# Three rounded passes for the scores and weighted sums of two layers, and norms shifted on ScalarE over whole tiles

## The chip, the cores and the metric

The kernel runs on one core of a Trainium2 chip. Its time is the device time of one launch in microseconds (us). TensorE (PE) multiplies matrices out of SBUF into the eight banks of PSUM. VectorE (DVE) and ScalarE (ACT) work elementwise on SBUF and PSUM, and both also empty the banks. SyncE (SP) issues the transfers from and to HBM. Every engine works through its own instructions in order, and semaphores tie the engines together.

## The reference

Four layers act on 256 latent tokens and 256 context tokens, 2048 wide: Fourier mixing, a bidirectional mLSTM with 8 heads, grouped-query attention with 16 heads on 4 key heads, and Fourier mixing again. Everything is in 32 bits. The parts that the change touches are, in short:

```
hx = rmsnorm(x, g) * (1 + scale) + shift        # before each layer, for both streams
# layer 1, mLSTM: per head (128 wide q, k; 256 wide v)
s   = (q @ k.T) * exp(decay - m)                # scores with decays
num = s @ v                                     # weighted sum of values
h   = num / max(|sum s|, exp(-m));  y = rmsnorm(sigmoid(o) * h) * silu(z)
# layer 2, attention: only the latent queries are needed
p   = softmax(q @ k.T / sqrt(128));  y = (p @ v) * silu(z)
```

## The kernel before, in words

**The large matmuls.** `gemm` multiplies the 16 blocks of 128 rows of the activations with a weight block of 512 columns. Each 32-bit number is split into a rounded part and the rest, both in the type fp32r (`h` and `l` for activations, `wh` and `wl` for weights). One product is then three passes: `h*wh`, `h*wl`, `l*wh` (line 308). For weights ScalarE makes the rounded part (L266) and VectorE the rest (L267). Work that is written as F32 on PE, without the split, is one matmul in the program and two instructions on the engine.

**Order of the work.** PE's order is the order of the program text. The other engines' order is set by a scheduler that looks at the program's dependences. `Weave` mixes small work into the large matmuls: `run(gemm(...), fr, br, ar)` gives `fr` steps of the generator queue `fill` and `br` steps of `bg` for each step of the gemm. A gemm's step is mostly the 6 passes of one of its blocks with two blocks of activations; a generator's step is its code up to the next `yield`. `fill.finish(key)` runs what is left at once. `bg` holds the products that make the layers' modulation vectors on VectorE (`ada_dve`, L227, 1024 columns each, about 1.2 us).

**Buffers.** The gemms use four PSUM banks (`acc`), one for each of their four blocks. A gemm's last step finishes its blocks one after the other, `done(b, ...)` empties bank `b`, and the next gemm needs bank `b` when it comes to its block `b`. The small work shares the other four banks (`xb`).

**Layer 1** works on four pairs of heads. Each pair has four gemms with the evictions `done_qk`, `done_v`, `done_o`, `done_z`. The first two are one ScalarE copy for a bank. `core` runs in the steps of the third and fourth gemm: for each of 8 tiles, `stage_a` computes the scores on PE (L846) and applies the decays on VectorE and ScalarE, `stage_b` turns the result on PE (L882) and copies it (`wt`), and `stage_c` multiplies it with the values (L891). `stage_a` runs one tile ahead. `finish` of a pair normalises, turns, and stores `zs` to HBM (L977) while the next pair's first gemm runs.

**Layer 2** has the gemms k, v, four q, four z. `qk_norm` normalises and rotates q or k and turns it (L1082) after four steps' wait. `attend` works on 8 tiles per key head: `stage_a` scores (L1097), a row maximum on VectorE (L1099), exponentials on ScalarE (L1103); `stage_b` turns (L1109) and `stage_c` multiplies with the values (L1118).

**Norms between layers.** `Norm.make` gives block `kt` of the next layer's input. `modulate` does it for one stream, 256 columns: VectorE scales (L405), ScalarE adds the shift and rounds (L406), VectorE makes the rest (L407). The first four blocks are made stream by stream, the other twelve for both.

Of the kernel before, what the change touches and what calls it, by code (L numbers as in the profile page):

```python
# [14 lines left out]
P = 128  # L15
# [9 lines left out]
NPE1, CORE1, ATT = 4, 0.4, 1.2  # L25
# [24 lines left out]
def _build(tc, nc, top, A, out):  # L50
# [360 lines left out]
    class Norm:  # L411
# [20 lines left out]
        def make(self, kt, s=None, have=None):  # L432
            for s in range(2) if s is None else (s,):
                have = modulate(self.l, kt, self.rn[kt // 4][:, kt % 4, 256 * s:256 * s + 256], self.rows[s],
                                self.pp, s, have)
            return have
# [304 lines left out]
    with ExitStack() as st:  # L741
        p1 = pool(st, "l1", reuse_waits="tile")

        def w2(name):
            return p1.tile([P, 512], F32, tag="w2", name=name, bufs=5)
# [6 lines left out]
        def gates():  # L752
# [21 lines left out]
            sb = pY.tile([P, 4, 512], F32, tag="zs", name="sb", bufs=1)  # L774
            ri, rl, rb, rM, z0 = sa[:, 0, :], sa[:, 1, :], sa[:, 2, :], sa[:, 3, :], sb[:, 0, :]
# [25 lines left out]
            for n, src in enumerate((ri, rM, rb)):  # L801
                r = sb[:, n + 1, :]
# [21 lines left out]
        def core(c):  # L824
# [16 lines left out]
            def stage_a(hh, i, ub, um):  # L841
# [4 lines left out]
                T.matmul(sp[:, :ns], c.qk[:, hh, dg], c.qk[:, 2 + hh, :ns], start=True, stop=True)  # L846
# [31 lines left out]
            def stage_b(hh, i, big):  # L878
                ns = 256 if i < 2 else 512
                pt = bank()  # L880
                for k in range(ns // 128):
                    T.transpose(pt[:, 128 * k:128 * k + 128], big[:, 128 * k:128 * k + 128], ident)  # L882
                wt = p1.tile([P, 512], F32, tag="wt", name="wt", bufs=2)
                S.copy(wt[:, :ns], pt[:, :ns])
                return wt

            def stage_c(hh, i, wt):
                nb = 2 if i < 2 else 4
                po = bank()
                for k in range(nb):  # L890
                    T.matmul(po[:, :256], wt[:, 128 * k:128 * k + 128], c.v[:, k, 256 * hh:256 * hh + 256],  # L891
                             start=k == 0, stop=k == nb - 1)
                ys = c.yp[:, i, 256 * hh:256 * hh + 256]
                if c.pend is not None:
                    S.copy(ys, po[:, :256])
                    c.pend.append((hh, i))
                else:
                    c.gate(hh, i, po[:, :256])
# [3 lines left out]
            w = {0: stage_a(0, 0, *u[0])}  # L902
            yield
            for n, (hh, i) in enumerate(tiles):
                if n == 2:
                    u[1] = load(1)
                if n + 1 < 8:
                    h2, i2 = tiles[n + 1]
                    w[n + 1] = stage_a(h2, i2, *u[h2])
                    yield  # L910
                if n:
                    stage_c(*tiles[n - 1], wt)
                    yield
# [24 lines left out]
        def make_pair(p):  # L938
            c = Pair()
            c.p = p  # L940
            c.qk = p1.tile([P, 4, 512], F32, tag="qk", name="qk", bufs=1)
            c.v = p1.tile([P, 4, 512], F32, tag="v", name="v", bufs=1)
            c.to = p1.tile([P, 4, 512], F32, tag="to", name="to", bufs=1)
            c.ssq = pY.tile([P, 8], F32, tag="ssq", name="ssq", bufs=2)
            c.pend = []

            def gate(hh, i, src):
                ys = c.yp[:, i, 256 * hh:256 * hh + 256]
                V.scalar_tensor_tensor(ys, c.to[:, i, 256 * hh:256 * hh + 256], 1.0, src, ALU.add, ALU.mult)  # L949
                jk = p1.tile([P, 256], F32, tag="jk", name="jk", bufs=1)  # L950
                S.activation(jk, ys, AF.Square, accum_out=c.ssq[:, 4 * hh + i:4 * hh + i + 1])  # L951

            c.gate = gate

            def done_qk(b, ps):
                S.activation(c.qk[:, b, :], ps, AF.Copy, scale=128 ** -0.5 if b < 2 else 1.0)

            def done_v(b, ps):
                S.copy(c.v[:, b, :], ps)

            def done_o(b, ps):
                S.activation(c.to[:, b, :], ps, AF.Tanh, scale=0.5)
                if b == 3:
                    pend, c.pend = c.pend, None
                    for hh, i in pend:
                        gate(hh, i, c.yp[:, i, 256 * hh:256 * hh + 256])
# [26 lines left out]
        for p in range(4):  # L993
# [9 lines left out]
            c.zs = pY.tile([P, 4, 512], F32, tag="zs", name="zs", bufs=1)  # L1003
# [38 lines left out]
    with ExitStack() as st:  # L1042
# [45 lines left out]
        def done_k(b, ps):  # L1088
            fill.add("kT", qk_norm(ps, 1, b - 2 if b >= 2 else None, kT[:, :, 128 * b:128 * b + 128]))
# [4 lines left out]
        def attend(g, qT, o):  # L1094
# [34 lines left out]
            yield  # L1129
# [31 lines left out]
        for g in range(4):  # L1161
            qT = p2.tile([P, 4, 256], F32, tag="qT", name="qT", bufs=2)
# [251 lines left out]
```

## Time and profile before

| | us |
|---|---|
| median of 3 runs | 2126.71 (2125.92 to 2127.11) |
| the profiled execution | 2128.92 |
| its span, first to last instruction | 2127.1 |
| PE busy in the span | 2083.3 |
| DVE, ACT busy | 1508.7, 817.8 |

A row with a window gives, for each engine, the busy time and in brackets the number of instructions. A row of the timeline gives the start and the duration in us, the engine, the line, and what is written and read. A matmul's duration reaches past the start of the next, because matmuls overlap in the array; what one costs is read from start to start. "x2" on a row of the timeline stands for two instructions in a row. A row of a group ends with the busy time of the group, the mean of one in ns, and the engine's idle time just before them with what ended it.

### The profile page before, as it was taken

To read this page: it belongs to the slowest core of one execution; us is meant where nothing else is said; L and a number is where in the kernel's file an instruction comes from. 1 tells how busy PE (TensorE), PEld (TensorE's weight loads), DVE (VectorE), ACT (ScalarE), POOL (GpSimd) and SP (SyncE) were. 2 spreads that over 40 slices of the span, in tenths; PEclk is the share of its full clock that TensorE was granted. 3 is DMA by queue.
4 is the path that set the end of the run, shared out by engine and by line. 5 is a ranking of instruction groups with operands and counts; after the bars stand their busy time and mean duration, and the time that the engine had idled before them with its cause. 6 is when DMAs were issued, how large, how long until landed. Compare 5 with 4: busy or idle time off the path is not lost. (4 is left out here: it accounts for less than half of the span.)

```text
span 2127.1 us, 29564 instructions
## 1 busy us (share of the span) xinstructions
PE 2083.3 (98%) x11292; PEld 1727.8 (81%) x11292; DVE 1508.7 (71%) x2761; ACT 817.8 (38%) x1342; POOL 20.4 (1%) x29
## 2 busy tenths in 40 slices
PE   7999999999999999999999999999999999999997
PEld 5678777797788888888888888888778777999986
DVE  6478888748787887798666768856545665657666
ACT  5442232224343324323332343223346554555443
POOL 0000000000000000000000000000000000000000
PEclk9999999999999999999999999999999999999999
DMA  9966878852554675477577778973243454564454
GB/s 395 333 242 210 293 256 302 323 191 96 179 188 163 221 244 169 162 272 248 186 240 262 236 239 299 334 288 107 89 148 111 151 176 131 184 194 136 150 198 148
DMA packets 127422, 451.51 MB, mean 212 GB/s; under 512 B 14368, under 2 KB 16928, under 8 KB 124592
## 3 DMA queue, kind: packets, MB, share of 16 engines
q1 hardware_dynamic: 126992, 448.71, 61.5%
q8 instruction: 88, 1.44, 0.3%
q10 hardware_dynamic: 288, 0.92, 0.1%
q14 instruction: 54, 0.44, 0.1%
HBM read 435.91 MB, written 13.66 MB: 211 GB/s over the span
## 5 line engine op out<-in xcount | busy, mean ns | idle before, releaser
L267 DVE TENSOR_TENSOR wl<-wraw,wh 128x1024 fp32r<-128x1024 f32 x400 | 489.1, 1224 | 405.5 <-ACT wh L266 398.2
L308 PE MATMUL acc<-h,wh 128*128 128x512 f32 (+1 forms) x1936 | 689.1, 356 | 6.6 <-ACT h L406 3.9
L266 ACT CAST wh<-wraw 128x1024 fp32r<-128x1024 f32 x400 | 419.3, 1049 | 701.2 <-PE acc L308 553.5
L308 PE MATMUL acc<-l,wh 128*128 128x512 f32 (+1 forms) x1936 | 671.4, 347 | 2.1 <-DVE l L407 1.8
L308 PE MATMUL acc<-h,wl 128*128 128x512 f32 (+1 forms) x1936 | 669.7, 346 | 0.1
L308 PE MATMUL acc<-wh,h 128*128 128x512 f32 x1024 | 426.8, 417 | 3.5 <-DVE xn L1062 2.2
L308 PEld LDWEIGHTS acc<-h,wh 128*128 128x128 f32 x1936 | 366.9, 190 | 66.3 <-issue 13.8
L308 PEld LDWEIGHTS acc<-l,wh 128*128 128x128 f32 x1936 | 366.7, 189 | 51.3 <-DVE l L407 3.5
L308 PEld LDWEIGHTS acc<-h,wl 128*128 128x128 f32 x1936 | 367.2, 190 | 44.0 <-issue 1.9
L308 PE MATMUL acc<-wh,l 128*128 128x512 f32 x1024 | 400.8, 391 | 0.5 <-DVE l L407 0.5
L308 PE MATMUL acc<-wl,h 128*128 128x512 f32 x1024 | 399.2, 390 | 0.0
L227 DVE SCALAR_TENSOR_TENSOR araw<-araw,cb 128x1024 f32<-128x1024 f32 x288 | 350.9, 1226 | 14.4 <-DMA araw<-in_ada_t_dram 12.1
L308 PEld LDWEIGHTS acc<-wh,h 128*128 128x128 f32 x1024 | 192.6, 188 | 51.8 <-issue 14.5
L308 PEld LDWEIGHTS acc<-wl,h 128*128 128x128 f32 x1024 | 192.8, 188 | 44.5 <-issue 8.4
L308 PEld LDWEIGHTS acc<-wh,l 128*128 128x128 f32 x1024 | 192.3, 188 | 42.7 <-DVE l L407 1.3
L227 DVE SCALAR_TENSOR_TENSOR ajunk<-araw,cb 128x1024 f32<-128x1024 f32 x160 | 195.6, 1223 | 0.0
L197 PE MATMUL xb<-araw,cpad 128*32 128x256 f32 x696 | 48.5, 396 | 4.4 <-ACT wh L266 2.6
L406 ACT ACTIVATE h<-mu,ada 128x256 fp32r<-128x256 f32 x80 | 36.9, 502 | 35.9 <-DVE mu L405 35.9
L891 PE MATMUL xb<-v,wt 128*128 128x256 f32 x192 | 46.8, 379 | 0.0
L464 ACT ACTIVATE sq<-rn 128x256 f32<-128x256 f32 (+1 forms) x48 | 24.7, 516 | 55.6 <-DVE rn L458 53.8
L951 ACT ACTIVATE jk<-yp 128x256 f32<-128x256 f32 x32 | 13.3, 416 | 79.8 <-DVE yp L949 79.8
L891 PEld LDWEIGHTS xb<-v,wt 128*128 128x128 f32 x192 | 36.4, 189 | 6.1
(231 smaller groups left out, 1480.3 us busy)
## 6 DMA issues: line engine op xcount, KB each, us to landing
araw<-in_ada_t_dram SPq DMA_DIRECT2D x288, 512.0 KB, 5.3
wraw<-in_w1in_dram SPq DMA_DIRECT2D x128, 512.0 KB, 4.3
araw<-in_ada_p_dram SPq DMA_DIRECT2D x87, 512.0 KB, 6.9
wraw<-in_w2in_dram SPq DMA_DIRECT2D x80, 512.0 KB, 3.5
wraw<-in_w0g_dram SPq DMA_DIRECT2D x32, 512.0 KB, 6.2
wraw<-in_w0o_dram SPq DMA_DIRECT2D x32, 512.0 KB, 6.1
wraw<-in_w1o_dram SPq DMA_DIRECT2D x32, 512.0 KB, 6.0
wraw<-in_w2o_dram SPq DMA_DIRECT2D x32, 512.0 KB, 4.1
```

The costliest lines, as they stand in the source:

```text
L197: T.matmul(ps[32 * q:32 * q + 32, :256], cpad[:, 4 * kq + q, :], rv[q // 2][:, 256 * (q % 2):256 * (q % 2) + 256], start=kq == 0, stop=kq ...
L227: V.scalar_tensor_tensor(o, rv, 1.0, cb[:, v + 2 - nv, part], ALU.mult, ALU.mult, accum_out=am[:, v, i, hf:hf + 1])
L266: S.copy(wh, raw)
L267: pace.append(V.tensor_tensor(wl, raw, wh.bitcast(F32), ALU.subtract).ins)
L308: T.matmul(o, lhsT, rhs, start=start, stop=stop)
L406: S.activation(h[:, c], u, AF.Identity, bias=ada[:, l, SH, s, kt:kt + 1])
L464: S.activation(sq[:, c], rn[:, b, c], AF.Square)
L891: T.matmul(po[:, :256], wt[:, 128 * k:128 * k + 128], c.v[:, k, 256 * hh:256 * hh + 256], start=k == 0, stop=k == nb - 1)
L951: S.activation(jk, ys, AF.Square, accum_out=c.ssq[:, 4 * hh + i:4 * hh + i + 1])
```

## The change

1. **Layer 1.** `done_qk` and `done_v` make, after ScalarE's copy, the rest on VectorE (`ql`, `vl`, 512 columns). Scores are three rounded passes in place of one F32 matmul, and so is each product of `stage_c`; `stage_b` therefore makes the rest `wtl` too. `stage_a` runs two tiles ahead, and `CORE1` is 0.56 steps instead of 0.4. `ql` shares its place with `zs`, so it waits for the store of the pair before, and `zs` for the end of this pair's `core`. The gate is written into `yp` itself.
2. **Layer 2.** `kT` and `qT` become rounded, their rests go to the context halves of input tiles in `hl` that are not read any more (`spare`), and a score is two passes of 512 columns and two of 256. Turning q waits six steps, a key head's second tile two steps more, and `ATT` is 1.35. The product with the values stays F32.
3. **Norms.** For the last twelve blocks VectorE multiplies by the row factor alone (256 columns), ScalarE applies scale and shift on the same place, then rounds 512 columns, and VectorE makes the rest of 512 columns.

```diff
-NPE1, CORE1, ATT = 4, 0.4, 1.2
+NPE1, CORE1, ATT = 4, 0.56, 1.35
...
         def make(self, kt, s=None, have=None):
...
+            u = self.pp.tile([P, 512], F32, tag="mu2", name="mu2", bufs=2)
+            for s in range(2):
+                c = slice(256 * s, 256 * s + 256)
+                V.tensor_tensor(u[:, c], self.rn[kt // 4][:, kt % 4, c], self.rows[s], ALU.mult)
+                S.activation(u[:, c], u[:, c], AF.Identity, scale=ada[:, self.l, SC, s, kt:kt + 1],
+                             bias=ada[:, self.l, SH, s, kt:kt + 1])
+            return split_into(kt, u)
...
-                T.matmul(sp[:, :ns], c.qk[:, hh, dg], c.qk[:, 2 + hh, :ns], start=True, stop=True)
+                for ip, (q, k) in enumerate(((c.qk, c.qk), (c.qk, c.ql), (c.ql, c.qk))):
+                    T.matmul(sp[:, :ns], q[:, hh, dg], k[:, 2 + hh, :ns], start=ip == 0, stop=ip == 2)
...
                 S.copy(wt[:, :ns], pt[:, :ns])
-                return wt
+                V.tensor_tensor(wtl[:, :ns], pt[:, :ns], wt[:, :ns].bitcast(F32), ALU.subtract)
+                return wt, wtl
...
-                    T.matmul(po[:, :256], wt[:, 128 * k:128 * k + 128], c.v[:, k, 256 * hh:256 * hh + 256],
-                             start=k == 0, stop=k == nb - 1)
+                    for ip, (w, v) in enumerate(((wt[0], c.v), (wt[0], c.vl), (wt[1], c.v))):
+                        T.matmul(po[:, :256], w[:, 128 * k:128 * k + 128], v[:, k, 256 * hh:256 * hh + 256],
+                                 start=k + ip == 0, stop=k == nb - 1 and ip == 2)
...
             def done_qk(b, ps):
-                S.activation(c.qk[:, b, :], ps, AF.Copy, scale=128 ** -0.5 if b < 2 else 1.0)
+                if b == 0:
+
+                    fill.finish(f"fin{p - 1}")
+                    c.ql = pY.tile([P, 4, 512], F32R, tag="zs", name="ql", bufs=1)
+                sc = 128 ** -0.5 if b < 2 else 1.0
+                S.activation(c.qk[:, b, :], ps, AF.Copy, scale=sc)
+                V.scalar_tensor_tensor(c.ql[:, b, :], ps, sc, c.qk[:, b, :].bitcast(F32), ALU.mult, ALU.subtract)
 
             def done_v(b, ps):
                 S.copy(c.v[:, b, :], ps)
+                V.tensor_tensor(c.vl[:, b, :], ps, c.v[:, b, :].bitcast(F32), ALU.subtract)
...
-                for _ in range(4):
+                for _ in range(4 if w else 6):
                     yield
...
+                for h in range(4):
+                    V.tensor_tensor(rest(h), pt[:, 128 * h:128 * h + 128], dst[:, h, :].bitcast(F32), ALU.subtract)
                 yield
...
-                T.matmul(sp, qT[:, hh, 128 * i:128 * i + 128], kT[:, g, :], start=True, stop=True)
+                t = slice(128 * i, 128 * i + 128)
+                T.matmul(sp, qT[:, hh, t], kT[:, g, :], start=True, stop=False)
+                T.matmul(sp, ql[hh][:, t], kT[:, g, :], start=False, stop=False)
+                for s in range(2):
+                    T.matmul(sp[:, 256 * s:256 * s + 256], qT[:, hh, t], kl[s], start=False, stop=s == 1)
...
             w, pts = {0: stage_a(0, 0)}, {}
-            yield
+            for _ in range(3):
+                yield
```

**Where instructions move, first place.** These are VectorE's rows before, in the first gemm of the second pair, some rows behind the last `zs` of the pair before; the `bg` pieces (L227) and the rests of the weights (L267) stand there:

```order
L227 SCALAR_TENSOR_TENSOR araw,am<-araw,cb 128x1024
L267 TENSOR_TENSOR wl<-wraw,wh 128x1024 x2
L227 SCALAR_TENSOR_TENSOR ajunk,am<-araw,cb 128x1024
L227 SCALAR_TENSOR_TENSOR araw,am<-araw,cb 128x1024
L227 SCALAR_TENSOR_TENSOR ajunk,am<-araw,cb 128x1024
```

And now, from the same place on (L971 is the rest of q and k, from a bank `acc`; the last three rows come twice more):

```order
L267 TENSOR_TENSOR wl<-wraw,wh 128x1024 x3
L227 SCALAR_TENSOR_TENSOR ajunk,am<-araw,cb 128x1024
L971 SCALAR_TENSOR_TENSOR ql<-acc,qk 128x512
L227 SCALAR_TENSOR_TENSOR araw,am<-araw,cb 128x1024
L227 SCALAR_TENSOR_TENSOR ajunk,am<-araw,cb 128x1024
L971 SCALAR_TENSOR_TENSOR ql<-acc,qk 128x512
```

Two `bg` pieces stand between one bank's rest and the next, four rests to a gemm; before, nothing on VectorE read these banks.

**Second place.** PE's rows before at the start of the second pair's `core`, with the gemm's passes (12 and 18 of them) left out:

```order
L846 MATMUL xb<-qk 128x256
...
L846 MATMUL xb<-qk 128x256
...
L882 MATMUL xb<-cst,eb 128x128 x2
```

And now:

```order
L853 MATMUL xb<-qk 128x256
L853 MATMUL xb<-ql,qk 128x256
L853 MATMUL xb<-qk,ql 128x256
...
L853 MATMUL xb<-qk 128x256
L853 MATMUL xb<-ql,qk 128x256
L853 MATMUL xb<-qk,ql 128x256
...
L889 MATMUL xb<-cst,eb 128x128 x2
```

The scores become three rows each, and between the second score and the first turn there are now 24 passes of the gemm instead of 18.

**Third place.** PE's rows before at the end of layer 2's last z gemm, where `attend` of the last key head is finished (L1118 is the product with the values; 12 passes of the gemm follow, left out; L1151 turns the outputs):

```order
L1109 MATMUL xb<-cst,pe 128x128 x4
L308 MATMUL acc<-wh,h_12589 128x512
...
L1118 MATMUL xb<-vv,pts 128x128 x8
...
L1151 MATMUL xb<-cst,o 128x128 x24
```

And now (L1146 is the turn, L1155 the product with the values, L1131 to L1134 the scores):

```order
L1131 MATMUL xb<-kT,qT 128x512
L1132 MATMUL xb<-kT,h_12776 128x512
L1134 MATMUL xb<-h_12656,qT 128x256
L1134 MATMUL xb<-l_12657,qT 128x256
L1146 MATMUL xb<-cst,pe 128x128 x4
L1155 MATMUL xb<-vv,pts 128x128 x4
L1131 MATMUL xb<-kT,qT 128x512
...
L1146 MATMUL xb<-cst,pe 128x128 x4
L1155 MATMUL xb<-vv,pts 128x128 x4
L1146 MATMUL xb<-cst,pe 128x128 x4
L1155 MATMUL xb<-vv,pts 128x128 x8
```

The last two tiles of the last key head now follow each other with no pass of a gemm between them.

## Rows read from the trace of the kernel before

**Rows 1.** Page, busy time of an engine: us, share of the span, instructions.
```profile
PE 2083.3 (98%) x11292; PEld 1727.8 (81%) x11292; DVE 1508.7 (71%) x2761; ACT 817.8 (38%) x1342; POOL 20.4 (1%) x29
```

**Rows 2.** Waits of PE: who waited for whom, us in total, times, longest.
```profile
PE acc L308 <- DVE l L407: 2.3, 4, 0.7
...
PE xb L1109 <- ACT pe L1103: 2.0, 2, 1.0
...
PE xb L1082 <- DVE rb L1074: 1.4, 2, 1.0
```

**Rows 3.** Groups by line and shape, PE, the F32 products that the change replaces.
```profile
L891 PE MATMUL xb<-v,wt 128*128 128x256 f32 x192 | 46.8, 379 | 0.0
...
L1097 PE MATMUL xb<-kT,qT 128*128 128x512 f32 x64 | 32.7, 592 | 0.0
...
L846 PE MATMUL xb<-qk 128*128 128x512 f32 x32 | 16.4, 593 | 0.0
...
L846 PE MATMUL xb<-qk 128*128 128x256 f32 x32 | 9.6, 380 | 0.0
```

**Rows 4.** Timeline, PE, 512-column score of layer 1, then 16 passes.
```profile
800.77 1.02 PE L846 MATMUL xb<-qk 128*128 128x512 f32 x2
...
801.87 0.40 PE L308 MATMUL acc<-wl,h 128*128 128x512 f32 x1
...
805.51 0.40 PE L308 MATMUL acc<-wh,l 128*128 128x512 f32 x1
```

**Rows 5.** Timeline, PE, around one 256-column score.
```profile
790.06 0.60 PE L846 MATMUL xb<-qk 128*128 128x256 f32 x2
...
790.73 0.40 PE L308 MATMUL acc<-wl,h 128*128 128x512 f32 x1
```

**Rows 6.** Timeline, PE, around two products of `stage_c`.
```profile
805.74 1.03 PE L891 MATMUL xb<-v,wt 128*128 128x256 f32 x4
...
806.83 0.40 PE L308 MATMUL acc<-wl,h 128*128 128x512 f32 x1
```

**Rows 7.** Timeline, PE, around one score of layer 2.
```profile
1592.61 1.02 PE L1097 MATMUL xb<-kT,qT 128*128 128x512 f32 x2
...
1593.71 0.40 PE L308 MATMUL acc<-wl,h 128*128 128x512 f32 x1
```

**Rows 8.** Timeline, PE, rounded passes of 256 columns, back to back.
```profile
1860.06 0.28 PE L308 MATMUL acc<-h,wh 128*128 128x256 f32 x1
1860.18 0.28 PE L308 MATMUL acc<-h,wl 128*128 128x256 f32 x1
```

**Rows 9.** Group, weight loads (PEld) of the rounded passes.
```profile
L308 PEld LDWEIGHTS acc<-h,wl 128*128 128x128 f32 x1936 | 367.2, 190 | 44.0 <-issue 1.9
```

**Rows 10.** Groups by line and shape, DVE.
```profile
L227 DVE SCALAR_TENSOR_TENSOR ajunk<-araw,cb 128x1024 f32<-128x1024 f32 x160 | 195.6, 1223 | 0.0
...
L407 DVE SCALAR_TENSOR_TENSOR l<-mu,ada,h 128x256 fp32r<-128x256 f32 x80 | 35.7, 481 | 5.8 <-ACT h L406 5.8
...
L1062 DVE TENSOR_TENSOR xn<-acc,r 128x512 f32<-128x512 f32 x12 | 8.3, 688 | 0.3
```

**Rows 11.** Window, third pair's first two gemms: PE, PEld, DVE, ACT, POOL busy, clock.
```profile
891.99:980.89 88.90, 88.90 (x401) 73.66 (x400) 82.33 (x136) 27.06 (x37) 0.00 (x0) 1.00 0.75 253
```

**Rows 12.** Timeline, SP and ACT: a pair's last store, the next eviction of `qk`.
```profile
720.74 0.33 SPq L977 DMA_DIRECT2D ytd<-zs  x1
...
734.49 0.60 ACT L956 ACTIVATE qk<-acc 128x512 f32<-128x512 f32 x1 [1.67 <-PE acc L308]
```

**Rows 13.** Instructions on tile `ytd`: landing of its transfers.
```profile
DMA to landing us min/median/max: 2.7/4.8/5.8
```

**Rows 14.** Groups by line and shape, ACT.
```profile
L266 ACT CAST wh<-wraw 128x1024 fp32r<-128x1024 f32 x400 | 419.3, 1049 | 701.2 <-PE acc L308 553.5 <-issue 61.5 <-DVE araw L227 25.8
...
L648 ACT ACTIVATE u<-xT,ada 128x256 f32<-128x256 f32 x32 | 17.6, 593 | 14.7 <-DVE ada L167 14.6
...
L371 ACT CAST h<-u 128x512 fp32r<-128x512 f32 x16 | 9.8, 611 | 0.2
```

More of the change, by code (lines that the diff above doesn't have):

```diff
@@ L432, in make @@
         def make(self, kt, s=None, have=None):
-            for s in range(2) if s is None else (s,):
-                have = modulate(self.l, kt, self.rn[kt // 4][:, kt % 4, 256 * s:256 * s + 256], self.rows[s],
+            if s is not None:
+                return modulate(self.l, kt, self.rn[kt // 4][:, kt % 4, 256 * s:256 * s + 256], self.rows[s],
                                 self.pp, s, have)
-            return have
+            u = self.pp.tile([P, 512], F32, tag="mu2", name="mu2", bufs=2)
[5 more added lines that the diff above has]
+            return split_into(kt, u)
     def out_proj(pp, px, l, hl, old, new_dram, c0, rates, tag="xf", bufs=5, gate=None, norm=None):
@@ L744, in w2 @@
         def w2(name):
-            return p1.tile([P, 512], F32, tag="w2", name=name, bufs=5)
+            return p1.tile([P, 512], F32, tag="w2", name=name, bufs=6)
         bgate = p1.tile([P, 1], F32, name="bgate")
@@ L773, in gates @@
             sa = pY.tile([P, 4, 512], F32, tag="yp", name="sa", bufs=1)
-            sb = pY.tile([P, 4, 512], F32, tag="zs", name="sb", bufs=1)
-            ri, rl, rb, rM, z0 = sa[:, 0, :], sa[:, 1, :], sa[:, 2, :], sa[:, 3, :], sb[:, 0, :]
+            sb = [w2(f"sb{n}") for n in range(4)]
+            ri, rl, rb, rM, z0 = sa[:, 0, :], sa[:, 1, :], sa[:, 2, :], sa[:, 3, :], sb[0]
             S.activation(ri[0:64, :], pg[0:64, :], AF.Identity, bias=bgate[0:64])
@@ L882, in stage_b @@
                     T.transpose(pt[:, 128 * k:128 * k + 128], big[:, 128 * k:128 * k + 128], ident)
-                wt = p1.tile([P, 512], F32, tag="wt", name="wt", bufs=2)
+                wt = p1.tile([P, 512], F32R, tag="wt", name="wt", bufs=2)
+                wtl = p1.tile([P, 512], F32R, tag="wtl", name="wtl", bufs=2)
                 S.copy(wt[:, :ns], pt[:, :ns])
-                return wt
+                V.tensor_tensor(wtl[:, :ns], pt[:, :ns], wt[:, :ns].bitcast(F32), ALU.subtract)
+                return wt, wtl
             def stage_c(hh, i, wt):
@@ L947, in gate @@
-            def gate(hh, i, src):
+            c.to, c.po = set(), set()
+            def gate(hh, i, to, src, junk=None):
                 ys = c.yp[:, i, 256 * hh:256 * hh + 256]
-                V.scalar_tensor_tensor(ys, c.to[:, i, 256 * hh:256 * hh + 256], 1.0, src, ALU.add, ALU.mult)
-                jk = p1.tile([P, 256], F32, tag="jk", name="jk", bufs=1)
-                S.activation(jk, ys, AF.Square, accum_out=c.ssq[:, 4 * hh + i:4 * hh + i + 1])
+                V.scalar_tensor_tensor(ys, to, 1.0, src, ALU.add, ALU.mult)
+                S.activation(src if junk is None else junk, ys, AF.Square, accum_out=c.ssq[:, 4 * hh + i:4 * hh + i + 1])
@@ L958, in done_v @@
             def done_v(b, ps):
                 S.copy(c.v[:, b, :], ps)
+                V.tensor_tensor(c.vl[:, b, :], ps, c.v[:, b, :].bitcast(F32), ALU.subtract)
             def done_o(b, ps):
[L962 to L966, printed above, removed]
+                for hh in range(2):
+                    cols = slice(256 * hh, 256 * hh + 256)
+                    ys = c.yp[:, b, cols]
+                    if (hh, b) in c.po:
+                        to = p1.tile([P, 256], F32, tag="to", name="to", bufs=1)
+                        S.activation(to, ps[:, cols], AF.Tanh, scale=0.5)
+                        gate(hh, b, to, ys, ps[:, cols])
+                    else:
+                        S.activation(ys, ps[:, cols], AF.Tanh, scale=0.5)
+                        c.to.add((hh, b))
@@ L968, in done_z @@
             def done_z(b, ps):
+                if b == 0:
+                    fill.finish(f"core{p}")
+                    c.zs = pY.tile([P, 4, 512], F32, tag="zs", name="zs", bufs=1)
                 tz = w2("tz")
@@ L1046, in w2, with spare, qk_norm @@
             return p2.tile([P, 512], F32, tag="w2", name=name, bufs=7)
-        kT = p2.tile([P, 4, 512], F32, name="kT")
+        def spare(kt0, n):
+            return [hl[kt0 + i // 2][i % 2][:, 0:256] for i in range(n)]
+        kT = p2.tile([P, 4, 512], F32R, name="kT")
         vv = p2.tile([P, 4, 512], F32, name="vv")
-        def qk_norm(ps, w, i, dst):
+        def qk_norm(ps, w, i, dst, rest):
             sq = w2("sq")
@@ L1161, in _build @@
         for g in range(4):
-            qT = p2.tile([P, 4, 256], F32, tag="qT", name="qT", bufs=2)
+            qT = p2.tile([P, 4, 256], F32R, tag="qT", name="qT", bufs=2)
+            ql = spare(4 + 2 * (g % 2), 4)
             o = pO.tile([P, 2, 512], F32, tag="oy", name="o", bufs=5)
@@ L1166, in done_q @@
             def done_q(b, ps):
-                fill.add("qT", qk_norm(ps, 0, b, qT[:, :, 128 * b:128 * b + 128]))
+                c = slice(128 * b, 128 * b + 128)
+                fill.add("qT", qk_norm(ps, 0, b, qT[:, :, c], lambda h, ql=ql: ql[h][:, c]))
             run(gemm(hl, "B", 256, 512, done_q), ATT, 0)
-            fill.add(f"att{g}", attend(g, qT, o))
+            fill.add(f"att{g}", attend(g, qT, ql, o))
         for g in range(4):
```

50 lines of the change are left out of this document (25 added, 25 removed).

## The prediction

> **What bounds the kernel now.** I read the busy times first: PE is busy for 2083.3 of the span's 2127.1 us [rows 1], and the granted clock is full (1.00) in the window shown [rows 11]. So the time is PE's work, and a change is worth what it takes from PE or adds to its waits. The waits of PE come next. The ones that the change can touch are small: 2.0 us for exponentials and 1.4 us for rotated q in layer 2, and 2.3 us for the rests that the norms make [rows 2]. Then I took the groups by shape for the count of each product that is replaced [rows 3], and the timeline for its price, start to start, since durations overlap [rows 4 to 8].
>
> **PE's work, term by term.** Sixteen rounded passes of 512 columns take 805.51 - 801.87 us, 0.227 each [rows 4]. A rounded pass of 256 columns costs 0.12 [rows 8]. An F32 product is two instructions, and its price is the time from its start to the start of the second rounded pass behind it, less one pass, 0.23 (the first pass behind it starts early and waits in the array).
> - Scores of layer 1 with 512 columns: 801.87 - 800.77 - 0.23 = 0.87 us [rows 4]. 32 instructions are 16 products [rows 3]. Three passes cost 0.68. 16 x 0.19 = 3.0 us saved.
> - Scores of layer 1 with 256 columns: 790.73 - 790.06 - 0.23 = 0.44 [rows 5]; three passes 0.36; 16 x 0.08 = 1.3 us saved.
> - Sums of values in layer 1: two products take 806.83 - 805.74 - 0.23 = 0.86, one 0.43 [rows 6]. 192 instructions are 96 products [rows 3]; three passes 0.36; 96 x 0.07 = 6.9 us saved.
> - Scores of layer 2: 1593.71 - 1592.61 - 0.23 = 0.87 [rows 7]; now 2 x 0.227 + 2 x 0.12 = 0.69; 32 products x 0.175 = 5.6 us saved.
>
> Together PE does 16.8 us less. No other matmul changes. Since PE runs without a gap around these places, all of it comes off the end unless a wait takes its place.
>
> A pass costs at least what rows 8 show, and at most the time of its weight load if loads do not overlap: 0.19 us [rows 9]. I take 0.12, because rows 8 are the same instruction in the same type, back to back. [...]
>
> **What the change adds on VectorE and ScalarE.** A rest from PSUM, 512 columns, is bounded by the row of the same kind, 0.69 us [rows 10]. Per pair of heads that is 8 rests for q, k and v, and 4 long and 4 short ones for `wtl` (short: at most the 0.48 of the 256-column row): 10.2 us, 41 us in all, beside 1508.7 busy [rows 1]. The 48 small rests of layer 2 cost at most 0.48 each, 23 us over a stage in which PE leads. All of it is hidden if it comes in time. Four places decide.
>
> *Seams of the first two gemms of a pair.* A bank is now read by ScalarE (0.60) and then VectorE (0.69). A block's end takes 12 passes, 2.72 us, and the next gemm reaches bank 3 after 18 passes, 4.1 us behind the end: 2.8 us are left. Between two rests VectorE has two modulation pieces, 2 x 1.22 plus their two short accumulator reads, some 2.5 us with 0.69 for the rest, 3.2 us against 2.72. So the fourth rest is late by 1.5 us, less than 2.8. Behind the rest on VectorE stand more such pieces and the weights' rests, which PE needs only one gemm step in two. The fullest stretch is the third pair's: VectorE is busy 82.3 of 88.9 us [rows 11], with 8 x 0.69 more it is 87.8, or 99%. Cost: 0 to 1 us at each of eight seams; I take 2 us for all, as only the fullest pair comes near.
>
> *The place of `ql`.* Its first rest waits for the store of `zs`. The last store is issued at 720.74 and lands within 5.8 us, at 726.5; the eviction starts at 734.49 [rows 12, 13]. Eight us of slack: nothing.
>
> *`core` and `attend`.* In `core`, 18 passes and a score, some 4.5 us, now lie between a turn and its product; the chain is ScalarE 0.60, VectorE 0.69. With a cast (1.05, rows 14) and two pieces (2.45) ahead it is 4.8, a few tenths late, seldom: 1 us. In layer 2 the waits for exponentials and for q (2.0 and 1.4 us, rows 2) should go, since two more steps of 1.36 us each stand in their place. What is late next is the end: the last two tiles follow each other without a pass between them, so a turn comes 2.0 us of PE work behind its score, while maximum and exponential need over 2.5. I take 2 us for two such turns (bounds 1 and 4).
>
> *Norms.* Per block VectorE had 4 x 0.48 and half a weight's rest, 2.5 us, against PE's 2.72; now 2 x 0.48 + 0.69 + 0.61 = 2.3. ScalarE has 2 x 0.59 + 0.61 + 0.52 = 2.3 [rows 14]. Both stay ahead of PE, VectorE a little further, so about half of the 2.3 us of waits for rests goes [rows 2]; the other half lies at the first four blocks, where the scheduler now puts two blocks' multiplications ahead. Gain 1.
>
> The waits: 3.4 + 1 gained, 2 + 1 + 2 lost. I book zero, with bounds of -7 and +9.
>
> **The sum.** The profiled execution took 2128.92 us, 1.8 beside its span and 2.2 above the median of the runs, 2126.71. 2128.9 - 16.8 = 2112.1, and at the median 2109.9: I predict 2110 us.
>
> **Rivals.**
> - *The chains get too tight.* `core`'s steps come at 0.56 instead of 0.4 per step of a gemm, and each product has one VectorE operation more in its chain. If 32 tiles wait 0.25 us each, 8 us go: 2118. For it: 4.8 against 4.5 us above. Against: both queues must be full at once, and PE waits nowhere in these stretches now (idle before L891 and L846 is 0.0, rows 3).
> - *VectorE falls behind at the seams, and the kernel is slower.* With three pieces between two rests, 3.8 + 0.69 = 4.5 us against 2.72, the fourth rest is 5.3 us late, 2.5 beyond the slack. At eight seams that is 20 us and a little more where two follow closely, say 24: 2134. It decides from a lag of 2.8 + 2.1 = 4.9 us at bank 3. For it: the 99%. Against: the order has two pieces, and only this pair is so full.
> - *Weight loads set the pace.* Passes of 256 columns at 0.19 us: sums of values 288 x 0.19 - 41.3 = +13.4, short scores 48 x 0.19 - 7.0 = +2.1, layer 2 32 x (0.83 - 0.87) = -1.3, long scores -3.0. Together +11.2: 2138. Against it are rows 8.
> - *The old waits go and no new one comes*: 7 us more, 2103.
>
> That the passes are not rounded ones at all I leave out: they have the type of line 308.
>
> **How the numbers follow.** Forecast 0.70, tight chains 0.16, no new wait 0.06, slower by VectorE 0.05, by loads 0.03. The range reaches from the lower bound to 9 us above the forecast: 2103 to 2119. A measurement of this kernel can tell 0.2%, 4.3 us, from no change. Faster by more: 0.70 + 0.06 + most of 0.16, 0.89. Within: 0.04. Slower: 0.07.
>
> **What would show it.** Right: groups of scores and sums without idle time before them, 48 + 48 + 288 + 128 rounded passes, an F32 group of neither, PE's busy time near 2065, no wait for `bg`-bound VectorE at the gemms behind q, k and v. Wrong: waits of PE for `ql`, `vl` or `wtl` of more than 5 us together, or passes of 256 columns spaced by more than 0.13. If these waits pass 21 us, the sign is wrong.

## The result and the profile after

The changed kernel takes 2110.82 us (median of 4 runs, 2109.32 to 2111.99) against 2126.91 beside it: a ratio of 0.992 (95% interval 0.9903 to 0.9937). The forecast was 2110. The executions profiled span 2127.1 us before and 2107.5 after, 19.6 apart; what that holds besides the change is below.

The page's busy time, the line that answers to [rows 1]:

```profile
PE 2063.6 (98%) x11484; PEld 1735.0 (82%) x11484; DVE 1541.0 (73%) x2849; ACT 847.1 (40%) x1390; POOL 19.3 (1%) x29
```

PE does 19.7 us less, VectorE 32 us and ScalarE 29 us more. Of PE's 19.7 us, 3.1 lie ahead of layer 1 (468.5 us busy before, 465.3 after), in code that the change does not touch. The prices of the new products, from PE's timeline (start in us, duration, line), answer to [rows 4, 6, 7]. A 512-column score of layer 1, a product of values (three passes to a product), and a score of layer 2, each with the gemm's pass behind it:

```profile
792.25 0.39 PE L853 MATMUL xb<-qk 128*128 128x512 f32 x1
...
792.94 0.39 PE L308 MATMUL acc<-wh,h 128*128 128x512 f32 x1
...
795.68 0.28 PE L901 MATMUL xb<-v,wt 128*128 128x256 f32 x1
795.80 0.28 PE L901 MATMUL xb<-vl,wt 128*128 128x256 f32 x1
...
796.39 0.39 PE L308 MATMUL acc<-wh,h 128*128 128x512 f32 x1
```

```profile
1577.32 0.39 PE L1131 MATMUL xb<-kT,qT 128*128 128x512 f32 x1
...
1578.02 0.40 PE L308 MATMUL acc<-wh,h 128*128 128x512 f32 x1
```

From the start of the first pass to the start of the gemm's pass behind, these are 0.69 us for a score (0.68 forecast), 0.71 for two products of values (0.72), and 0.70 for a score of layer 2 (0.69). The passes of 256 columns stand 0.12 apart.

PE's waits (who for whom; us in total, times, longest) answer to [rows 2]:

```profile
PE acc L308 <- ACT h L406: 4.0, 4, 1.1
...
PE acc L308 <- DVE wl L267: 2.5, 1, 2.5
...
PE acc L308 <- DVE xn L1089: 1.4, 1, 1.4
PE acc L308 <- DVE zs L995: 1.4, 1, 1.4
...
PE xb L1146 <- ACT pe L1140: 1.1, 3, 0.5
PE acc L308 <- DVE l L407: 0.8, 1, 0.8
```

The waits for rotated q are gone, those for exponentials are 1.1 us instead of 2.0, those for the norms' rests 0.8 instead of 2.3. Two are new: 2.5 us for a weight's rest (`wl`) and 1.4 us for an eviction of z (`zs`).

Where the span changed is seen by cutting it at the gemms that begin layer 1, its output gemms, layer 2 and its output gemms. The windows of before and of after (from and to, then the width; PE's busy time and instructions follow, as in [rows 11]):

```profile
485.88:1281.83 795.95, 792.10 (x3607) 645.04 (x3606) 611.18 (x1174) 280.34 (x483) 20.22 (x25) 1.00 0.63 209
1281.83:1461.96 180.13, 180.13 (x988) 156.82 (x986) 123.78 (x215) 47.70 (x62) 0.00 (x0) 1.00 0.76 275
1461.96:1815.67 353.71, 345.24 (x1684) 277.27 (x1683) 213.90 (x312) 174.34 (x273) 0.00 (x0) 1.00 0.41 133
```

```profile
484.72:1266.19 781.47, 779.50 (x3734) 645.79 (x3733) 636.75 (x1232) 298.45 (x520) 19.14 (x25) 1.00 0.64 212
1266.19:1447.75 181.56, 180.17 (x988) 156.83 (x987) 124.27 (x211) 47.19 (x59) 0.00 (x0) 1.00 0.76 277
1447.75:1796.10 348.35, 341.28 (x1748) 286.95 (x1747) 220.16 (x348) 186.19 (x287) 0.00 (x0) 1.00 0.42 135
```

Layer 1 is 14.5 us shorter, its output gemms 1.4 longer, layer 2 5.4 shorter; from there to PE's last instruction it is 300.6 us in both. The stretch ahead of layer 1, which the change does not touch, is 1.2 shorter (484.72 against 485.88). In layer 2 the 32 scores are some 5 us cheaper by their prices (0.87 us before, 0.70 to 0.71 now), yet PE's busy time fell by 4.0 only. That does not fit the forecast's working and led to the experiments.

What happens around the 2.5 us wait is on VectorE's timeline, in the last of layer 2's four gemms for q (L1084 to L1101 are the norm and rotation of a block of q, L1112 the small rests):

```profile
1622.53 1.23 DVE L267 TENSOR_TENSOR wl<-wraw,wh 128x1024 fp32r<-128x1024 f32 x1 [1.82 <-ACT wh L266]
...
1627.92 0.29 DVE L1112 TENSOR_TENSOR h<-xb,qT 128x128 fp32r<-128x128 f32 x1
...
1629.92 0.28 DVE L1112 TENSOR_TENSOR l<-xb,qT 128x128 fp32r<-128x128 f32 x1
1630.12 0.28 DVE L1112 TENSOR_TENSOR h<-xb,qT 128x128 fp32r<-128x128 f32 x1
1630.32 0.28 DVE L1112 TENSOR_TENSOR l<-xb,qT 128x128 fp32r<-128x128 f32 x1
1631.39 0.18 DVE L1086 RECIPROCAL r<-r 128x4 f32<-128x4 f32 x1 [0.79 <-ACT r L1085]
1631.48 1.20 DVE L267 TENSOR_TENSOR wl<-wraw,wh 128x1024 fp32r<-128x1024 f32 x1
```

Between two weights' rests lie 8.9 us. Ahead of the second stand the norm of one block of q and the start of the next one's, the four small rests of another block (0.2 us each, start to start), and a reciprocal that waits 0.79 us for ScalarE. The rounded part that this rest needs was done at 1627.28, 4.2 us before the rest began (row of ScalarE):

```profile
1626.25 1.03 ACT L266 CAST wh<-wraw 128x1024 fp32r<-128x1024 f32 x1
```

PE takes the next weight from this rest:

```profile
1632.73 0.50 PE L308 MATMUL acc<-wl,h 128*128 128x512 f32 x1 [2.48 <-DVE wl L267]
...
1634.04 0.63 PE L308 MATMUL acc<-wh,l 128*128 128x512 f32 x1
1634.47 0.63 PE L308 MATMUL acc<-wh,h 128*128 128x512 f32 x1
```

Soon after it the passes stand 0.43 us apart instead of 0.227: the clock has fallen. The window's last columns are the granted clock (0.52 of full), the DMA share and GB/s:

```profile
1633.62:1637.00 3.38, 3.38 (x10) 2.70 (x9) 3.13 (x4) 0.00 (x0) 0.00 (x0) 0.52 0.81 211
```

The wait and the slow passes cost 2.5 + 1.9 us: from the last pass ahead of the wait, at 1629.87, to the first that is followed at the old spacing, at 1636.94, 12 passes take 7.1 us, and at 0.227 each they would take 2.7.

### The profile page after: what moved, and what is told of

Read it like the earlier page. It is cut to its first block, busy times and chain, and to the rows that moved or that the text cites. A ratio compares the mean times of both kernels' runs of the same rounds, so it can differ in the third digit from the quotient of the medians.

```text
span 2107.5 us, 30089 instructions
## 1 busy us (share of the span) xinstructions
PE 2063.6 (98%) x11484; PEld 1735.0 (82%) x11484; DVE 1541.0 (73%) x2849; ACT 847.1 (40%) x1390; POOL 19.3 (1%) x29
## 4 chain that ended last, share of the span: by engine, by line
PE 94%; DVE 3%; DMA 1%; ACT 1%; issue 1%; SPq 0%; ACTq 0%; DVEq 0%
PE acc L308 82%; PE xb L197 2%; PE xb L901 2%; PE xb L1155 1%; PE xb L515 1%; PE xb L548 1%; PE xb L853 1%; DMA araw<-in_ada_p_dram 1%; PE xb L1146 1%; PE xb L889 0%; DVE wl L267 0%; PE xb L770 0%; PE xb L1134 0%; DMA lraw<-in_ada_p_dram 0%; PE xb L941 0%
## 5 line engine op out<-in xcount | busy, mean ns | idle before, releaser
L267 DVE TENSOR_TENSOR wl<-wraw,wh 128x1024 fp32r<-128x1024 f32 x400 | 488.6, 1223 | 364.5 <-ACT wh L266 355.0
L308 PE MATMUL acc<-h,wh 128*128 128x512 f32 (+1 forms) x1936 | 681.2, 352 | 7.1 <-ACT h L406 3.0
L308 PE MATMUL acc<-wh,h 128*128 128x512 f32 x1024 | 408.5, 399 | 2.4 <-DVE xn L1089 1.4
L227 DVE SCALAR_TENSOR_TENSOR araw<-araw,cb 128x1024 f32<-128x1024 f32 x288 | 349.4, 1221 | 9.9 <-DMA araw<-in_ada_t_dram 8.8
L227 DVE SCALAR_TENSOR_TENSOR ajunk<-araw,cb 128x1024 f32<-128x1024 f32 x160 | 196.5, 1228 | 0.0
L1136 DVE TENSOR_REDUCE mx<-xb 128x1 f32<-128x512 f32 x32 | 22.1, 689 | 30.3 <-PE xb L1134 30.1
L464 DVE SCALAR_TENSOR_TENSOR rn<-acc,ada,rold 128x256 f32<-128x256 f32 x80 | 36.0, 480 | 6.8 <-PE acc L308 6.6
L197 PEld LDWEIGHTS xb<-araw,cpad 128*32 128x32 f32 x696 | 19.3, 111 | 25.5 <-DMA araw<-in_ada_p_dram 6.1
L1155 PEld LDWEIGHTS xb<-vv,pts 128*128 128x128 f32 x256 | 32.5, 192 | 1.8
```

Of the source, the lines that this page charges most:

```text
L197: T.matmul(ps[32 * q:32 * q + 32, :256], cpad[:, 4 * kq + q, :], rv[q // 2][:, 256 * (q % 2):256 * (q % 2) + 256], start=kq == 0, stop=kq ...
L227: V.scalar_tensor_tensor(o, rv, 1.0, cb[:, v + 2 - nv, part], ALU.mult, ALU.mult, accum_out=am[:, v, i, hf:hf + 1])
L267: pace.append(V.tensor_tensor(wl, raw, wh.bitcast(F32), ALU.subtract).ins)
L308: T.matmul(o, lhsT, rhs, start=start, stop=stop)
L464: V.scalar_tensor_tensor(rn[:, b, a:a + 256], ps[:, 256 * s - o:256 * s - o + 256], ada[:, l, GA, s, kt:kt + 1], ro[:, b, a:a + 256], ALU. ...
L1155: T.matmul(po[i][:, 128 * hh:128 * hh + 128], pts[:, 128 * k:128 * k + 128], vv[:, k, 128 * g:128 * g + 128], start=k == 0, stop=k == 3)
```

## The experiments

The spans of layer 1 and layer 2 repeat within 0.15 us in the three traces of the changed kernel (781.33 to 781.47, 348.35 to 348.40), while the stretch ahead of layer 1 varied from 484.2 to 490.5 us over all traces, the first block of layer 3 between 25.9 and 27.5, and the runs of one kernel by 2 to 11 us. So the verdicts rest on spans; the ratios to the kernel before stand beside them.

**The products as F32 again, the rest of the change kept.** The same edit in scores, sums and layer 2:

```diff
-                for ip, (q, k) in enumerate(((c.qk, c.qk), (c.qk, c.ql), (c.ql, c.qk))):
-                    T.matmul(sp[:, :ns], q[:, hh, dg], k[:, 2 + hh, :ns], start=ip == 0, stop=ip == 2)
+                T.matmul(sp[:, :ns], c.qk[:, hh, dg], c.qk[:, 2 + hh, :ns], start=True, stop=True)
...
-                V.tensor_tensor(c.vl[:, b, :], ps, c.v[:, b, :].bitcast(F32), ALU.subtract)
```

> The changed kernel with all three kinds of products as F32 again and no rests for them (no ql, vl, wtl, no small rests in layer 2); its order of steps, its rates and its norms stay. Theory (PE's work sets the time): the 16.8 us come back on PE, busy 2063.6 + 16.8 = 2080.4 us, time 2110.8 + 16.8 = 2127.6 us; or 2123.3, if the 2.5 us wait at 1632.73 and the half clock behind it (4.3 us together) go with the small rests. Rival (the new order of steps and rates gave the gain, not the passes): 2111 to 2115 us.

Measured: 2122.9 us, ratio 0.9953 (0.9939 to 0.9966), PE busy 2081.8. Windows of layer 1 and layer 2:

```profile
487.51:1280.37 792.86, 790.88 (x3607) 644.98 (x3606) 609.06 (x1169) 298.82 (x520) 16.45 (x25) 1.00 0.63 209
...
1460.85:1809.00 348.15, 344.18 (x1684) 277.56 (x1683) 210.72 (x300) 186.46 (x287) 0.00 (x0) 1.00 0.42 135
```

Layer 1 gives back 11.4 us, what its products were priced at (11.2 in the forecast). Layer 2 gives back nothing: 348.15 against 348.35. That fits the second of the two times expected, 2123.3 us. The rival (order and rates made the gain, not the passes) falls for layer 1; in layer 2 the passes brought nothing, and the gain came from the rest of the change.

**Only layer 2's scores as F32.** The scores and the four small rests of `turn` go:

```diff
...
-                for h in range(4):
-                    V.tensor_tensor(rest(h), pt[:, 128 * h:128 * h + 128], dst[:, h, :].bitcast(F32), ALU.subtract)
...
-                T.matmul(sp, qT[:, hh, t], kT[:, g, :], start=True, stop=False)
-                T.matmul(sp, ql[hh][:, t], kT[:, g, :], start=False, stop=False)
-                for s in range(2):
-                    T.matmul(sp[:, 256 * s:256 * s + 256], qT[:, hh, t], kl[s], start=False, stop=s == 1)
+                T.matmul(sp, qT[:, hh, t], kT[:, g, :], start=True, stop=True)
...
```

> The changed kernel with the scores of layer 2 alone as F32 again, without their small rests. Theory: 32 products cost 0.862 - 0.706 us more each, +5.0, so 2115.8 us; 2111.5 if the wait at 1632.73 goes with the rests; layer 1 keeps its spans to 0.5 us. Rival (order and rates): no change in the stretch of layer 2.

Measured: 2113.15 us, ratio 0.9911 (0.9897 to 0.9924), as that of the changed kernel. Layer 2 takes 348.19 us, and PE no longer waits for a weight's rest there. Its busy time is 344.23 us against 341.28 with rounded passes. Those 341.28 hold 1.9 us of slow clock, so the work fell by 4.9 us and the span by nothing: 2.5 us went to the wait, 1.9 to the slow clock, and 0.8 to waits for exponentials (1.1 against 0.3). In the same gemm for q, a weight's rest now stands where the first small rest stood, behind the product of L1096, and 5.4 us after the one before it:

```profile
1630.82 1.22 DVE L267 TENSOR_TENSOR wl<-wraw,wh 128x1024 fp32r<-128x1024 f32 x1
```

So the four small rests cost little by their own time on VectorE, 0.2 us each; with them and the rounded scores in the program, the weight's rest was put behind the whole batch.

**The norms undone**, in the changed kernel, and **the norms alone**, the same edit the other way, in the kernel before:

```diff
-            if s is not None:
-                return modulate(self.l, kt, self.rn[kt // 4][:, kt % 4, 256 * s:256 * s + 256], self.rows[s],
+            for s in range(2) if s is None else (s,):
+                have = modulate(self.l, kt, self.rn[kt // 4][:, kt % 4, 256 * s:256 * s + 256], self.rows[s],
                                 self.pp, s, have)
-            u = self.pp.tile([P, 512], F32, tag="mu2", name="mu2", bufs=2)
-            for s in range(2):
-                c = slice(256 * s, 256 * s + 256)
-                V.tensor_tensor(u[:, c], self.rn[kt // 4][:, kt % 4, c], self.rows[s], ALU.mult)
-                S.activation(u[:, c], u[:, c], AF.Identity, scale=ada[:, self.l, SC, s, kt:kt + 1],
-                             bias=ada[:, self.l, SH, s, kt:kt + 1])
-            return split_into(kt, u)
+            return have
```

> The changed kernel with the norms between the layers as before (scale and shift on VectorE in half tiles). By the forecast (half of the waits for rests goes by this edit): +1 us, 2112 us. By the two traces (waits of 2.9 us behind 503 us and of 1.4 us behind 1501 us that are gone after the change): +4.3 us, 2115 us. Rival (hidden anyway): 2110.8 us, and the waits do not come back.

Measured: 2116.01 us, ratio 0.9927 (0.9914 to 0.9939). Layer 1 takes 784.23 us (+2.8, in its first gemm: 51.15 against 48.25) and layer 2 350.39 (+2.0, in the gemms for k and v): the 4.8 us of the traces, not the forecast's 1. The waits are back:

```profile
PE acc L308 <- ACT h L406: 5.2, 6, 1.1
...
PE acc L308 <- DVE l L407: 2.3, 4, 0.7
PE acc L308 <- DVE xn L1083: 2.2, 1, 2.2
```

These are 3.5 us above those after (4.0, 0.8 and 1.4). In the kernel before, the first two rows read the same, and the third is this:

```profile
PE acc L308 <- DVE xn L1062: 2.2, 1, 2.2
```

The other 1.4 us of the run with the norms undone stand in PE's busy time (780.40 and 341.76 us in the two layers, against 779.50 and 341.28).

> The kernel before with the edit of the norms alone. Theory (the edit is worth the same with and without the rounded passes, 4.8 us in the spans of three gemms): the first gemm of layer 1 takes 48.2 us instead of 51.1, those for k and v of layer 2 47.5 and 47.1 instead of 48.8 and 47.9; all other spans stay; ratio 0.9977. Rival (the forecast's half of 2.3 us): ratio 0.9995. Rival (the gain needs VectorE's other changes): spans as before.

Measured: 2124.39 us, ratio 0.9968 (0.9957 to 0.998). The three gemms take 48.23, 47.43 and 47.12 us instead of 51.14, 48.75 and 47.88: 5.0 us. The edit is worth the same with rounded passes and without. Its windows of layer 1 and layer 2 also show, beside those of the F32 run, what order and rates are worth (neither kernel makes a rest of q, k, v or `wt`):

```profile
484.31:1277.34 793.03, 791.06 (x3606) 645.03 (x3605) 607.76 (x1162) 288.88 (x495) 18.67 (x25) 1.00 0.63 210
...
1457.47:1809.01 351.54, 344.63 (x1684) 277.25 (x1682) 210.47 (x300) 183.26 (x285) 0.00 (x0) 1.00 0.41 134
```

From 793.03 to 792.86 it is 0.2 us in layer 1; from 351.54 to 348.15 it is 3.4 in layer 2, the size of the waits for exponentials and rotated q that went.

**A fourth pass in the sums of values.** Each of the 96 products gets a fourth pass, rest by rest:

```diff
-                    for ip, (w, v) in enumerate(((wt[0], c.v), (wt[0], c.vl), (wt[1], c.v))):
+                    for ip, (w, v) in enumerate(((wt[0], c.v), (wt[0], c.vl), (wt[1], c.v), (wt[1], c.vl))):
...
```

> The changed kernel with a fourth pass (rest by rest) in every product of the sums of values in layer 1: 96 passes of 256 columns more. Theory (a pass costs its columns, 0.12 us, the load lies beside it): +11.5 us, 2122.3 us. Rival (a pass costs its weight load, 0.19 us): +18.2 us, 2129.0 us. Third way (these stretches wait for VectorE, so that a pass more fills a gap): under +6 us.

Measured: 2119.22 us, ratio 0.9945 (0.9932 to 0.9957). Layer 1 takes 792.92 us, 11.45 more: 0.119 for each added pass.

```profile
484.97:1277.89 792.92, 790.95 (x3830) 656.57 (x3829) 638.32 (x1233) 300.24 (x520) 18.35 (x25) 1.00 0.63 209
```

With it PE loads 96 more weights, 190 ns each by their records, and they cost nothing of their own. The rival by weight loads is refuted for these products.

**Every rest of q, k and v made three times.** 4.5 us of VectorE work then lie between two blocks, the condition of the forecast's rival on the other side:

```diff
...
-                V.tensor_tensor(c.vl[:, b, :], ps, c.v[:, b, :].bitcast(F32), ALU.subtract)
+                for _ in range(3):
+                    V.tensor_tensor(c.vl[:, b, :], ps, c.v[:, b, :].bitcast(F32), ALU.subtract)
```

> The changed kernel with every rest of q, k and v in layer 1 made three times over (the same values): 16 VectorE operations of 0.6 to 0.69 us more per pair of heads, and 4.5 us of VectorE work between two blocks that end 2.72 us apart, as in the rival of the forecast in which VectorE falls behind at the seams. By that rival: 2.5 us of wait at each of eight seams, 20 us, 2131 us. By shares alone: only the third pair overflows (84.3 + 16 x 0.65 = 94.7 us of work in 88.9 us), +6 us, 2117. By a lag that the next gemm takes up: under +2 us.

Measured: 2130.09 us (2125.64 to 2136.16, 12 runs), ratio 0.9993 (0.9982 to 1.0004): the whole gain is gone. Layer 1 takes 800.56 us, 19.1 more. PE's waits are for the rests themselves and for weights' rests behind them; the window that follows the longest, 3.6 us at 744.61, has the low clock again, 0.57 of full:

```profile
PE acc L308 <- DVE ql L972: 7.5, 3, 3.6
PE acc L308 <- DVE wl L267: 4.5, 6, 2.5
...
PE acc L308 <- DVE vl L977: 2.6, 3, 1.7
```

```profile
745.00:749.00 4.00, 4.00 (x12) 3.13 (x11) 4.00 (x6) 1.05 (x1) 0.00 (x0) 0.57 0.60 193
```

So the rival's mechanism is real. Its price of 20 us is met in sum only, and not by 2.5 us at each of eight seams: the second and third pairs pay 7.1 and 7.9 us in the two gemms behind their q, k and v, the first and last 1.7 and 2.6. It is not the shares that decide: in the changed kernel VectorE is busy for 77.2 of the second pair's first 89.0 us, and 11 us more would just fit, yet it pays nearly as much as the third. Without the added rests no such wait stands: in the changed kernel the first two gemms of a pair (from the second pair on) take the 45.4 and 43.5 us of before.

**Seven steps instead of six before a block of q is turned**, with the changed kernel again as yardstick:

```diff
-                for _ in range(4 if w else 6):
+                for _ in range(4 if w else 7):
```

> The changed kernel once more, as the yardstick beside the next three. If the wait of 2.5 us for a weight's rest in the last gemm for q of layer 2 (fourth head group) and the half clock behind it belong to the order of instructions on VectorE, they are there again, and that gemm takes 34.8 us; if they were a chance of one execution, it takes about 31.3. Ratio to the kernel before 0.992.

> The changed kernel with seven steps instead of six between a block of q in layer 2 and its turn, which takes the block of small rests apart on VectorE: a weight's rest then stands ahead of the second block's reciprocal. Theory (the small rests of one head group and the norm of the next queue ahead of the weight's rest that PE waits for): the 2.5 us wait and the half clock behind it go, the fourth gemm for q takes 31.3 us instead of 34.8, and the time falls by 3.5 us, ratio to after 0.9983. Rival (it is the weight's landing or its cast that is late): the wait stays, the time is that of the changed kernel.

Measured: 2110.52 us, ratio 0.9898 (0.9884 to 0.9912), for the yardstick, whose 2.5 us wait is there again and whose gemm takes 34.84 us. With seven steps it is 2108.8, ratio 0.9895 (0.9882 to 0.9907). Its gemm for q takes 29.04 us. That is less than expected because the kernel also moves steps to later gemms, so layer 2 as a whole is the measure: 345.15 us, 3.2 less. The wait has shrunk to 0.9 us, and the clock stays full behind it; the waits for exponentials are 1.5 us instead of 1.1.

```profile
1448.51:1793.66 345.15, 339.31 (x1748) 285.40 (x1746) 220.13 (x348) 185.77 (x287) 0.00 (x0) 1.00 0.43 136
```

On VectorE a weight's rest now stands in the first block's norm, behind L1096, as in the run with F32 scores, and the rest that is next follows 3 us behind:

```profile
1628.17 0.69 DVE L1096 TENSOR_TENSOR rb<-xn,tab 128x512 f32<-128x512 f32 x1
1628.78 1.22 DVE L267 TENSOR_TENSOR wl<-wraw,wh 128x1024 fp32r<-128x1024 f32 x1
...
1631.71 0.17 DVE L1086 RECIPROCAL r<-r 128x4 f32<-128x4 f32 x1
1631.80 1.20 DVE L267 TENSOR_TENSOR wl<-wraw,wh 128x1024 fp32r<-128x1024 f32 x1
```

So the order on VectorE made the wait, not the weight's landing or its cast, which was done 4.2 us before the late rest began. In the rows of the changed kernel this rest, ready to be made for 4.2 us, starts only 0.09 us after the start of the reciprocal ahead of it.

**Fewer pieces of modulation in the last gemm for z of layer 1**, on top of the seven steps. There PE waits 1.4 us for an eviction, ahead of which VectorE has pieces (L227) and a weight's rest; the third and the fourth eviction in the changed kernel:

```profile
1266.16 0.68 DVE L995 SCALAR_TENSOR_TENSOR zs<-tz,acc 128x512 f32<-128x512 f32 x1
1266.76 1.22 DVE L227 SCALAR_TENSOR_TENSOR araw<-araw,cb 128x1024 f32<-128x1024 f32 x1
...
1267.91 1.22 DVE L267 TENSOR_TENSOR wl<-wraw,wh 128x1024 fp32r<-128x1024 f32 x1
1269.04 0.68 DVE L995 SCALAR_TENSOR_TENSOR zs<-tz,acc 128x512 f32<-128x512 f32 x1
```

```diff
-BR1 = ((0, 0.35, 0.25, 0.25), (0.35, 0.35, 0.25, 0.25), (0.4, 0.4, 0.3, 0.3), (0.5, 0.5, 0.35, 0.35))
+BR1 = ((0, 0.35, 0.25, 0.25), (0.35, 0.35, 0.25, 0.25), (0.4, 0.4, 0.3, 0.3), (0.5, 0.5, 0.35, 0.2))
```

> As the seven-step kernel, and besides the modulation pieces are given at 0.2 instead of 0.35 a step in the last gemm for z of layer 1. Theory (pieces of modulation stand ahead of the eviction that PE waits for at the first output gemm): the wait of 0.7 to 1.9 us for zs there goes and that gemm takes 45.7 us as before the change; 1 to 3 us less than the seven-step kernel. Rival (the evictions are late for ScalarE's table load or for load_y's rests): that gemm stays at 46.4 to 49 us.

Measured: 2107.65 us, ratio 0.9894 (0.9881 to 0.9906). The first output gemm takes 45.62 us, as before the change (45.64), and the wait is gone.

> The version with seven steps and fewer modulation pieces in the last gemm for z again, beside the changed kernel on the same chip. From the spans of its stages 1.5 us less in the output gemms and 3.2 us less in layer 2 than the changed kernel: ratio to it 0.998. Rival (what is won in these stages is lost at the start, whose spans vary by some us): ratio 1.

> The changed kernel as the yardstick beside the two others: ratio to the kernel before 0.990 to 0.992.

Measured on another chip: 2107.77 us, ratio 0.9892 (0.9877 to 0.9907), against 2111.41, ratio 0.9906 (0.9892 to 0.992), for the changed kernel. The output gemms are 1.0 and 1.4 us shorter than in the changed kernel beside them, layer 2 is 3.2 us shorter both times, and the medians are 2.9 and 3.6 us lower. The intervals overlap, so by the times alone the lead is not shown.

## Why the prediction was right

The time came out within a microsecond, and that is luck in good part. The scores of layer 2 brought 5.8 us less than was booked, the norms brought 3.9 us more, and costs of 3 us in layer 1 and 2 in layer 2 did not come. The gain was 16.1 us by the medians of the result, where the kernel before had 2126.91; beside medians of 2131.87 and 2130.97 in two later series it was 21.4 and 19.6. Booked in the forecast and measured, in us (the measured column by spans, from the pair of kernels named):

| step | booked | measured |
|---|---|---|
| layer 1's products, with the rests at the seams and in `core` | -11.2 + 2 + 1 | -11.4 (F32 run and after) |
| layer 1's order and rates | 0 | -0.2 (norms alone and F32 run) |
| layer 2's scores, with their small rests | -5.6 | +0.2 (layer 2 as F32 and after) |
| norms | -1 | -4.9 (norms alone -5.0, undone -4.8) |
| layer 2's order and rates: old waits, new burst | -3.4 + 2 | -3.4 (norms alone and F32 run) |
| output gemms of layer 1 | 0 | +1.4 (windows) |
| ahead of layer 1 | 0 | -1.2 (untouched code) |
| sum | -16.2 | -19.5 |

The forecast rounded its waits to zero and took 16.8. The sum of the measured column is, to 0.1, the difference of the two profiled spans, 19.6. The medians differ by 16.1: the profiled execution of before lay 2.0 us above its median, that of after 1.5 below.

- *PE's work.* Right, term by term: by the rows above scores cost 0.69 and 0.70 us and two products of values 0.71, and passes of 256 columns stand 0.12 apart. That PE's busy time fell to 2063.6 (near 2065 was forecast) shows less: 3.1 of its 19.7 us lie in the untouched code ahead of layer 1. That weight loads, 190 ns by their records, do not set the spacing was taken from rows 8 and 9; the fourth pass, 0.119 us each, showed it for these products.
- *Layer 2's 5.6 us.* This step failed: "The 48 small rests of layer 2 cost at most 0.48 each, 23 us over a stage in which PE leads. All of it is hidden if it comes in time." The rests were counted by their time over the stage, and where they would stand on VectorE was not looked up. In one gemm for q they stand, with one block's norm and the start of another's, ahead of the weight's rest that PE needs next. Four rests take 0.8 us there, but with them the weight's rest began 8.9 us after the one before it instead of 5.4. The wait and the slow clock behind it took 4.4 of the 5 us.
- *Norms.* The direction was right and the size wrong. "... about half of the 2.3 us of waits for rests goes": the span lost 4.9. The forecast read the row of the rests (L407) alone. In the same stretches PE also waited for the halves that ScalarE made from VectorE's products (L406: 5.2 us before, 4.0 after) and, in the gemm for v, for evictions (2.2 and 1.4).
- *Steps in layer 2.* The 3.4 us of old waits went as said. The burst at the end, booked at 2, cost one wait of 0.33 us, at 1788.30. The turn there starts 1.9 us after the last pass of its score, so maximum and exponential did not need the "over 2.5" of the forecast. The other 0.8 of the 1.1 us of waits for exponentials stand at 1595 and 1602 us.
- *Seams of q, k and v, `ql`, `core`.* Booked 3, measured nothing: no wait for `ql`, `vl` or `wtl`, and the products of layer 1 gave all of their price. The lag that decides was judged rightly (3.2 us of VectorE work between two blocks fit, 4.5 do not), as the threefold rests show. But a ninth seam, from z to the output gemms, was not on the list, and there an eviction was late by 1.4 us (0.7 to 1.9 in the other traces with rounded products in layer 1 and the same pieces, 0.3 in the F32 run).

What was likeliest in the forecast (PE's saving with waits in balance) holds as a total, not term by term. Why the scheduler puts the weight's rest behind the whole batch in one gemm for q and not in the other three is not explained here.

## What to carry to other kernels

An operation that is hidden by its engine's average share is hidden only if nothing that the busiest engine needs next stands behind it in that engine's order, as the weight's rest did for which PE waited 2.5 us here: list the order at the two or three tightest seams. Adding a few short operations can move a long one: 0.8 us of small rests pushed a weight's rest back by some 3.5 us. Price a stall of one engine with all rows that its lateness feeds, not with the row that bears its name. A forecast that hits the time is shown right only when its terms are measured one by one.

## What was not expected of the hardware

A wait of PE can cost more than its length, and not always. Behind single waits of 1.9, 2.5 and 3.6 us the granted clock fell for some 3 us, to means of 0.71, 0.52 and 0.57 of full over windows of 4.0, 3.4 and 4.0 us; behind single waits of 1.4, 1.7 and 2.2 us it stayed at 1.00. Two equal waits need not agree: the 2.5 us wait in the gemm for q was followed by a clock of 1.00 in the run with threefold rests, and layer 2 took 346.80 us there instead of 348.35. What decides is not settled by these runs. The stretches at the waits of 1.9 us (layer 2 as F32, an eviction of z), of 1.4 (the same place in the changed kernel) and behind that of 2.5 with threefold rests:

```profile
1270.00:1274.00 4.00, 3.31 (x10) 2.58 (x11) 4.00 (x8) 0.00 (x0) 0.00 (x0) 0.71 0.87 286
```

```profile
1269.00:1273.00 4.00, 3.22 (x14) 2.68 (x15) 4.00 (x8) 0.00 (x0) 0.00 (x0) 1.00 0.95 270
```

```profile
1651.00:1655.00 4.00, 4.00 (x22) 3.31 (x20) 4.00 (x6) 1.06 (x1) 0.00 (x0) 1.00 0.67 209
```

The first of these gemms took 49.24 us and the second 47.08, against 45.64 without a wait: 3.6 us for a wait of 1.9, 1.4 for one of 1.4.

The traces hold a plainer case. In the first block of layer 3 every one of the 13 traces has the same two waits, of 0.84 to 0.85 and 0.74 to 0.75 us, less than a microsecond apart. Behind them the clock fell in eight traces and stayed full in five, and the block took 27.4 to 27.5 us in the eight and 25.9 in the five. The stretch behind them in the F32 run and after, with the granted clock (0.60 and 1.00) in the third column from the end:

```profile
1930.00:1934.00 4.00, 4.00 (x23) 4.00 (x23) 2.77 (x11) 0.87 (x3) 0.00 (x0) 0.60 0.41 135
```

```profile
1917.00:1921.00 4.00, 4.00 (x35) 4.00 (x34) 2.87 (x11) 1.34 (x4) 0.00 (x0) 1.00 0.41 131
```
